# Layer two's projections as seven block products of scaled float16 pairs in a two-layer decoder trunk

## The chip, the cores and the metric

The kernel runs on one core of one Trainium2 chip. The metric is the device time of one execution in microseconds (us), lower is better. Engines are named as the profile names them: PE is TensorE (PEld its weight loads), DVE is VectorE, ACT is ScalarE, POOL is GpSimd, SP is SyncE, whose queue issues the DMAs.

## The reference

Two decoder layers over 1024 tokens of width 1024 (batch 1), all in float32. Layer one mixes by causal pooling, layer two by gated "forgetting" attention over keys and values that are projected once from layer one's result. Both also attend to 256 memory tokens. Cut to what matters:

```python
def mixer_sublayer(x, mem, w_in, w_mem_kv, w_out, main_fn):
    h = x @ w_in                       # columns [main | mem q | main gate | mem gate]
    u_main, q_mem, g_main, g_mem = ...  # 1024, 512, 1024, 512 columns
    y_main = main_fn(u_main)
    y_mem = memory_attention(q_mem, mem, w_mem_kv)
    y = jnp.concatenate([y_main * jax.nn.silu(g_main), y_mem * jax.nn.silu(g_mem)], axis=-1)
    return y @ w_out

def reference(...):
    for layer in range(2):
        if layer == 0: main_fn = causal_multiscale_pool      # windows 2, 4, 8, 16
        else:
            k, v, cum = shared_kv(x, w_kv_shared, b_forget)  # 1024 + 1024 + 16 columns
            main_fn = forgetting_attention(k, v, cum)        # 16 heads of 64, causal, logit + cum[t] - cum[s]
        y = mixer_sublayer(x, mem, w_in[layer], w_mem_kv[layer], w_out[layer], main_fn)
        x = layer_norm(ALPHA * x + y, ln_g[layer], ln_b[layer])
```

## The kernel before

**Products.** Every float32 operand is a pair: a large part rounded to fp32r and a small part in bfloat16 (`hi_lo`: ACT casts the large part, L187, DVE subtracts, L188). A product of two operands is three matmuls, large by large in fp32r and two crossed ones in bfloat16 (`three`).

**Slabs.** A projection is cut into slabs of 128 output columns (`slab`, its matmuls are L253). A slab is 2 halves of 512 tokens x 8 blocks of 128 along the inner dimension x 3 = 48 matmuls with 512 columns each, accumulated in one of two banks `pj`. Its weights come in two DMAs of 256 KB into `raw` and are split into `w` and `wl`; while attention runs, the flag `low` gives both steps of the split to POOL (`gp_hi_lo`, L197, L198). Layer two has 38 slabs: 8 of memory queries and gates, 8 of keys, 8 of queries, 6 of values, 8 of gates. The values of the first two pairs of heads and the forget gates come from `v_first` (L733), with tokens as rows.

**Stages.** Layer one: four pooling groups (each two slabs of values, the pooling on DVE, two slabs of gates, and a small product L231), with the memory attention after the first, then the output projection (`OutProj`, L486) in row blocks of 256 tokens x 3 parts of 48 matmuls, `norm` (L537 to L550) and the transposes that make layer two's x (L348, ACT and POOL split it again). Layer two: memory keys and values, four slabs of memory queries, the memory attention (`probs` L388 to L399) with the gates' slabs between its products, then the start (keys and queries of pair 0, keys of pair 1, `v_first`, forget gates), then FoX, then the output projection.

**FoX.** `fox` runs over 16 heads x 8 query tiles. For a tile, `probs` makes the logits (L231, two fp32r matmuls for each part of at most 512 keys, into one of three banks `L`), DVE adds the forget rows and takes the extreme (L871), ACT exponentiates into one of two banks `T` (L879), and a tile later `inverse_of` (DVE, L889 to L892) and `halves` write the large half (ACT, L900) and the small half (DVE, L901) of the probabilities, which a transposing DMA (L913) turns for the product with the values (L926, L932, bank `O`, evacuated by L938 on ACT and L939 on DVE). POOL masks the rows (L863). Key and query slabs are evacuated by an ACT cast and a DVE subtraction on 64 partitions for each half head (L782, L783 and L792, L793); the swapped copies of the keys are made by DMA. Between these steps `fill.pump` puts a share of the coming slabs' matmuls on PE.

**Order.** PE's order is written out by hand (`manual_schedule`, and in FoX the constants SHARE, FRAC and LAG). The other engines' orders and the DMA queue's are laid by the framework's scheduler when the kernel is built. `OutProj.open` hands each row block four banks, from `pj`, `L`, `T` and `O` in turn.

## Time and profile before

| | |
|---|---|
| runs | 1224.68, 1230.59, 1228.9 us; median 1228.9 |
| profiled execution | 1224.89 us, its span 1223.2 us |
| granted PE clock | 0.997 |
| HBM read / written | 94.97 MB / 22.61 MB |

How to read the views: the busy time of a group of instructions is given with its count and the mean of one in ns, and behind a second bar the idle time of its engine just before it with what ended most of it. A matmul's own duration contains the time that its result takes to come out, so the pace is read from the starts of neighbours. A row of the waits says which engine and line waited, for which, how long in total, how many times, and the longest.

### The profile page before, as it was taken

To read this page: it belongs to the slowest core of one execution; us is meant where nothing else is said; L and a number is where in the kernel's file an instruction comes from. 1 tells how busy PE (TensorE), PEld (TensorE's weight loads), DVE (VectorE), ACT (ScalarE), POOL (GpSimd) and SP (SyncE) were. 2 spreads that over 40 slices of the span, in tenths; PEclk is the share of its full clock that TensorE was granted. 3 is DMA by queue.
4 is the path that set the end of the run, shared out by engine and by line. 5 is a ranking of instruction groups with operands and counts; after the bars stand their busy time and mean duration, and the time that the engine had idled before them with its cause. 6 is when DMAs were issued, how large, how long until landed. Compare 5 with 4: busy or idle time off the path is not lost. (4 is left out here: it accounts for less than half of the span.)

```text
span 1223.2 us, 19702 instructions
## 1 busy us (share of the span) xinstructions
PE 1193.1 (98%) x7018; PEld 749.0 (61%) x7018; DVE 787.3 (64%) x1861; ACT 607.2 (50%) x1318; POOL 201.8 (16%) x312
## 2 busy tenths in 40 slices
PE   9999999999999998999999999999999999999996
PEld 4567665555556557566775656666666666655553
DVE  6544776375554458257555878777878878775653
ACT  6433754263421135156334777767766777683110
POOL 2000000000000004000004334433334324530000
PEclk9999999999999999999999999999999999999998
DMA  6332454243363235224528698868887879975430
GB/s 238 115 104 93 115 121 147 87 121 97 126 208 104 103 104 190 69 77 99 173 64 167 161 177 182 194 148 188 184 178 174 185 175 226 232 232 175 163 113 35
DMA packets 267410, 178.65 MB, mean 146 GB/s; under 512 B 212272, under 2 KB 225712, under 8 KB 267312
## 3 DMA queue, kind: packets, MB, share of 16 engines
q1 hardware_dynamic: 267312, 177.40, 55.1%
q8 instruction: 55, 0.90, 0.3%
q14 instruction: 43, 0.35, 0.1%
HBM read 94.97 MB, written 22.61 MB: 96 GB/s over the span
## 5 line engine op out<-in xcount | busy, mean ns | idle before, releaser
L253 PE MATMUL pj<-A,w 128*128 128x512 bf16 (+1 forms) x1952 | 618.1, 398 | 2.2 <-DVE MK L340 0.9
L253 PE MATMUL pj<-A,wl 128*128 128x512 bf16 x976 | 369.1, 380 | 0.3 <-POOL A L192 0.3
L253 PEld LDWEIGHTS pj<-A,w 128*128 128x128 f32 x976 | 180.7, 188 | 46.0 <-ACT A L187 1.7
L253 PEld LDWEIGHTS <-w 128*128 128x128 bf16 x992 | 95.8, 98 | 123.8 <-issue 36.3
L253 PEld LDWEIGHTS <-wl 128*128 128x128 bf16 x992 | 97.4, 98 | 94.3 <-issue 6.1
L879 ACT ACTIVATE T<-MK,s 128x512 f32<-128x512 f32 x192 | 111.0, 578 | 57.1 <-DVE s L871 36.3
L901 DVE SCALAR_TENSOR_TENSOR P<-T,s,P 128x512 f16<-128x512 f32 x192 | 111.9, 613 | 32.8 <-ACT P L900 31.4
L900 ACT ACTIVATE P<-T,s 128x512 f16<-128x512 f32 x192 | 102.6, 575 | 51.2 <-issue 27.5
L188 DVE TENSOR_TENSOR wl<-raw,w 128x512 bf16<-128x512 f32 x98 | 71.0, 728 | 82.3 <-ACT w L187 81.7
L486 PEld LDWEIGHTS <-T 128*128 128x128 bf16 x736 | 70.8, 98 | 86.5 <-issue 3.9
L231 PE MATMUL L<-B,B 128*128 128x512 f32 (+3 forms) x384 | 110.8, 390 | 4.1 <-DVE s L871 3.8
L187 ACT CAST w<-raw 128x512 fp32r<-128x512 f32 x106 | 64.7, 617 | 99.8 <-PE pj L253 71.5
L231 PEld LDWEIGHTS L<-B,B 128*128 128x128 f32 x384 | 70.6, 189 | 30.7 <-DVE s L871 11.3
L192 POOL TENSOR_SCALAR A<-A 128x512 bf16<-128x512 f32 (+1 forms) x20 | 17.0, 866 | 433.5 <-ACT A L187 433.5
L871 DVE CUSTOM_DVE_ANT_0 MK<-L,R 128x512 f32<-128x512 f32 (+3 forms) x128 | 72.7, 568 | 8.1 <-DMA R<-cumd 4.4
L863 POOL TENSOR_SCALAR_AFFINE_SELECT R<-R 128x128 f32<-128x128 f32 x128 | 41.5, 330 | 212.5 <-DVE s L871 112.8
L187 ACT CAST T<-T 128x1024 fp32r<-128x1024 f32 x23 | 24.0, 1045 | 98.5 <-DMA T<-y1d 53.3
L198 POOL TENSOR_TENSOR wl<-raw,w 128x512 bf16<-128x512 f32 x54 | 69.1, 1280 | 3.5
L188 DVE TENSOR_TENSOR T<-T,T 128x1024 bf16<-128x1024 f32 x23 | 29.0, 1261 | 41.6 <-ACT T L187 21.7
L197 POOL TENSOR_SCALAR w<-raw 128x512 fp32r<-128x512 f32 x54 | 34.3, 634 | 71.6 <-PE pj L253 71.6
L231 PE MATMUL pj<-T,w 128*128 128x256 bf16 (+1 forms) x256 | 44.3, 281 | 1.5 <-DVE MK L340 1.5
L926 PE MATMUL O<-T,V 128*128 128x128 f16 x576 | 38.2, 219 | 4.9 <-DMA T<-P 4.9
(255 smaller groups left out, 1732.7 us busy)
## 6 DMA issues: line engine op xcount, KB each, us to landing
raw<-in_win_dram SPq DMA_DIRECT2D x96, 256.0 KB, 2.8
raw<-in_wout_dram SPq DMA_DIRECT2D x40, 256.0 KB, 2.7
B<-B SPq DMA_DIRECT2D x32, 256.0 KB, 4.4
R<-cumd SPq DMA_DIRECT2D x16, 512.0 KB, 4.3
y0d<-Y SPq DMA_DIRECT2D x12, 512.0 KB, 2.8
T<-y0d SPq DMA_DIRECT2D x12, 512.0 KB, 3.9
T<-y1d SPq DMA_DIRECT2D x11, 512.0 KB, 3.8
raw<-in_wmk_dram SPq DMA_DIRECT2D x16, 256.0 KB, 2.6
```

Source lines behind the costliest of these rows:

```text
L187: pin(nc.scalar.copy(hi, src))
L188: pin(by.tensor_tensor(lo[0], src, hi.bitcast(F32), ALU.subtract))
L198: nc.gpsimd.tensor_tensor(lo[0], src, hi.bitcast(F32), ALU.subtract)
L231: nc.tensor.matmul(acc, a, b, start=i == 0, stop=i == len(terms) - 1)
L253: nc.tensor.matmul(acc, a, b, start=start, stop=stop)
L486: nc.tensor.matmul(acc, y, w, start=c == 2 and j == firsts[id(acc)], stop=c == 1 and j == lasts[id(acc)])
L863: nc.gpsimd.affine_select(R[:, qs], R[:, qs], [[-1, P]], ALU.is_ge, -NEG, base=0, channel_multiplier=1).ins
L871: nc.vector.tensor_tensor_reduce(p[:, lo:up], lg, R[:, lo:up], 1.0, top, ALU.add, ALU.min, m[:, n : n + 1])
L879: nc.scalar.activation(e, p[:, lo:up], AF.Exp, bias=top, scale=-1.0, accum_out=sums[:, n, hd % 2, i : i + 1],)
L900: nc.scalar.activation(pair[:, lo:up], e, AF.Copy, scale=r)
L901: nc.vector.scalar_tensor_tensor(pair[:, L + lo : L + up], e, r, pair[:, lo:up], ALU.mult, ALU.subtract)
L926: nc.tensor.matmul(acc[:, cols(i)], v[:, b, 2 * j : 2 * j + 2, :].rearrange("p e d -> p (e d)"), pt[hd, i][:, j, :], start=n == 0, stop=Fa ...
```

## The change

Layer two's slabs are computed two at a time. The 1024 inner rows and the 2 x 128 columns of two slabs form 2 x 2 blocks of the weights, and x, with the inner dimension and the tokens cut in halves, 2 x 2 blocks too. Instead of 8 block products of 12 matmuls there are 7 (`strassen`, the form of Winograd with four sums on each side), whose results are combined in PSUM and in a tile U: a copy from bank to bank, two copies to U on ACT, two additions on DVE. All operands of these products are pairs of float16 parts, scaled by powers of two; the scales go back in where results leave PSUM.

- The four sums of x (T1 to T4) are made by POOL behind `norm`, and transposed with the four plain blocks (`turned`): 128 transposes where there were 64.
- The sums of the weight blocks are made in layer one by `prepass`, 20 groups, one started every 8 steps (`tick`) of PE's written order: four loads, a pass on ACT that measures the size, a small matmul that shares it over the partitions, a scaling on DVE, sums and halves on POOL and ACT, and seven stores of 256 KB to DRAM (`wd`). In layer two, `Stream` loads the blocks, four ahead.
- FoX has 14 groups, in the order FOX_GROUPS and to the goals TARGETS. The weight splits on POOL, the late gates and their reloads are gone. The swapped keys are made by POOL copies instead of DMAs.
- Banks: `pj` 3 (were 2), `L` 3, `T` 2; `O` is gone, its users take `L`. `raw`, `w` and `wl` share ten buffers.
- The rows of layer one's output projection go in blocks s and s + 4; `v_first` stands ahead of the memory queries and uses float16 pairs; the start has one group (keys and queries of pair 0). Layer one's keys and values of memory are called from the same code, and layer two's memory parts are loaded during layer one's last step.
- The scheduler lays the other engines' orders against another timing model (`schedule_with_timeline_sim=True`).

```diff
+ORDER = (B11, T1, T2, B21, T3, B22, T4)
+AHEAD = 4
+PERIOD = 8
+GROUP = 84 * NH
+PART = 12 * NH
+TARGETS = [2 * (p + 1) * GROUP + PART for p in range(5)] + [int(n * GROUP) for n in (11.6, 13.2, 14)]
...
+        def measure(m, first, raws):
+            for j, r in enumerate(raws):
+                r = flat(r)
+                nc.scalar.activation(junk[:, : r.shape[1]], r, AF.Abs, accum_out=m[:, first + j : first + j + 1])
...
+        def shared(diag):
+            t = ps([P, 4, P], "T", 2)
+            nc.tensor.matmul(t[:, 0, :], ones_b, diag, start=True, stop=True)
+            return t
...
+        def scale(k, t, raws):
+            e, sc = tiny(1), tiny(1)
+            nc.vector.tensor_reduce(e, t[:, 0, :], AX.X, ALU.max)
...
+            for r in raws:
+                nc.vector.tensor_scalar(r, r, sc, None, ALU.mult)
+        def large(src):
+            t = pre([P, 2, *src.shape[1:]], F16)
+            nc.scalar.copy(t[:, 0], src)
+            return t
+        def small_part(t, src):
+            nc.gpsimd.tensor_tensor(t[:, 1], src, t[:, 0], ALU.subtract)
+        def both(src):
+            t = pre([P, 2, *src.shape[1:]], F16)
+            nc.gpsimd.tensor_scalar(t[:, 0], src, 1.0, 1.0, ALU.mult, ALU.mult)
+            small_part(t, src)
+            return t
+        def group(k):
...
+            a11, a12, a21, a22 = r
+            s1 = pre()
+            nc.gpsimd.tensor_tensor(s1, a21, a22, ALU.add)
+            t22 = large(a22)
+            small_part(t22, a22)
+            yield
+            t11 = large(a11)
+            ts1 = both(s1)
+            yield
+            nc.sync.dma_start(wd[k, 6], t22)
+            nc.gpsimd.tensor_tensor(a21, a11, a21, ALU.subtract)
+            small_part(t11, a11)
...
+    def strassen(stream, XB, U, evac, straight=None, done=None):
+        def part(acc, k, fresh):
+            w = stream.block()
+            for kt in range(4):
+                for j, (a, b) in enumerate(((0, 0), (1, 0), (0, 1))):
+                    nc.tensor.matmul(
+                        acc, w[:, a, kt, :], XB[b][:, ORDER[k], kt, :], start=fresh and kt == 0 and j == 0,
+                        stop=kt == 3 and j == 2, skip_group_check=True,
+                    )
...
+        def summed(f, acc):
+            dst = straight(f) if straight else U[:, f, :]
+            nc.vector.tensor_tensor(dst, acc, U[:, f, :], ALU.add)
+            if not straight:
+                evac(f, slice(NH, S), dst)
+        b1 = bank()
+        yield from part(b1, 0, True)
+        b2 = bank()
+        nc.scalar.copy(b2, b1)
+        b3 = bank()
+        yield from part(b3, 1, True)
+        nc.scalar.copy(U[:, 1, :], b3)
+        yield from part(b2, 2, False)
+        nc.scalar.copy(U[:, 0, :], b2)
+        yield from part(b1, 3, False)
+        evac(0, slice(0, NH), b1)
+        yield from part(b2, 4, False)
+        summed(1, b2)
+        yield from part(b3, 5, False)
+        summed(0, b3)
+        yield from part(b2, 6, False)
+        evac(1, slice(0, NH), b2)
...
-            turned = ((pj, pj, l, l), (t, t, l, o)) if self.l else ((pj, pj, l, l), (l, o, pj, pj), (l, l, l, o))
+            turned = ((pj, l, pj, l), (t, t, pj, l)) if self.l else ((pj, l, pj, l),)
...
+    def turned(sp, zs, XB, sums):
+        (p0, p1), (s0, s1) = ((z[:, :NH], z[:, NH:]) for z in zs)
+        t1, t2, t3, t4 = sums
+        nc.gpsimd.tensor_tensor(t1, s0, p0, ALU.subtract)
+        nc.gpsimd.tensor_tensor(t2, s1, t1, ALU.subtract)
+        nc.gpsimd.tensor_tensor(t3, s1, s0, ALU.subtract)
+        nc.gpsimd.tensor_tensor(t4, p1, t2, ALU.subtract)
+        def turn(src, k):
+            t = ps([P, 4, P], "T", 2)
+            for j in range(4):
+                nc.tensor.transpose(t[:, j, :], src[:, j * P : (j + 1) * P], ident)
+            at = slice(None), k, slice(None), slice(sp * P, (sp + 1) * P)
+            nc.scalar.activation(XB[0][at], t, AF.Copy, scale=sx)
+            nc.vector.scalar_tensor_tensor(XB[1][at], t, sx, XB[0][at], ALU.mult, ALU.subtract)
...
-                        for to, of in ((own, other), (other, own)):
-                            nc.sync.dma_start(w[to, :].bitcast(F32), t[of, :].bitcast(F32))
+                for t, w, (own, other) in zip(ks, ws, halves) if f == 0 else ():
+                    for to, of in ((own, other), (other, own)):
+                        nc.gpsimd.tensor_scalar(w[to, cols], t[of, cols].bitcast(F32), 1.0, 1.0, ALU.mult, ALU.mult)
...
-            acc = ps([P, NH], "O", 1)
+            acc = ps([P, NH], "L", 3)
...
-    with _tile.TileContext(nc) as tc:
+    with _tile.TileContext(nc, schedule_with_timeline_sim=True) as tc:
```

More of the change, by code (lines that the diff above doesn't have):

```diff
@@ new lines, in trunk_kernel, with __init__, ahead, block @@
+    class Stream:
+        def __init__(self, groups):
+            self.blocks = [wd[k, i] for k in groups for i in range(7)]
+            self.tiles, self.n = [], 0
+        def ahead(self, upto):
+            for b in self.blocks[len(self.tiles) : upto]:
+                self.tiles.append(wt([P, 2, 4, P], F16))
+                nc.sync.dma_start(self.tiles[-1], b)
+        def block(self):
+            self.n += 1
+            self.ahead(self.n + AHEAD)
+            return self.tiles[self.n - 1]
@@ L376, in probs @@
+        ys = [ytile() for _ in range(MH)]
         def probs(i):
@@ L498, in early, with rest @@
             yield from self.products(self.accs, 2, yh, yl)
-        def rest(self, resid, XH, XL, dst):
-            self.split(24)
+        def rest(self, resid, XB, dst, last=None):
             gb = []
@@ L841, in start_units @@
             yield from own
-            complete(0)
         masked = []
```

676 lines of the change are left out of this document (433 added, 243 removed).

## The prediction

> **What bounds the kernel now.** I read four views, from coarse to fine: the page, the table of busy time by stage, the waits of each engine inside the longest stage, and the timeline of TensorE. From the page:
>
> ```profile
> span 1223.2 us, 19702 instructions
> PE 1193.1 (98%) x7018; PEld 749.0 (61%) x7018; DVE 787.3 (64%) x1861; ACT 607.2 (50%) x1318; POOL 201.8 (16%) x312
> ```
>
> TensorE looks like the bound everywhere. The stages, cut at layer one, layer two's memory attention, the start of its main path, the 128 attention tiles (FoX below), and the output projection (columns: stretch, length, then busy us and count of PE, PEld, DVE, ACT, POOL, the granted clock, DMA share, GB/s):
>
> ```profile
> 14.00:480.00 466.00, 463.61 (x2476) 284.58 (x2474) 271.39 (x496) 186.76 (x364) 20.90 (x24) 1.00 0.39 123
> 490.00:594.00 104.00, 104.00 (x642) 65.31 (x642) 54.23 (x134) 50.70 (x139) 0.00 (x0) 1.00 0.36 87
> 594.00:657.00 63.00, 63.00 (x408) 45.33 (x407) 30.30 (x75) 18.18 (x35) 4.46 (x7) 1.00 0.46 127
> 657.00:1081.00 424.00, 412.82 (x2752) 266.68 (x2750) 337.63 (x974) 300.89 (x699) 160.98 (x264) 1.00 0.84 185
> 1081.00:1223.00 142.00, 130.94 (x648) 75.93 (x648) 77.43 (x138) 34.63 (x59) 8.11 (x8) 0.98 0.42 140
> ```
>
> In the first three and the last, VectorE (DVE) is busy at most 58% of the time and TensorE all of it: there a matmul saved is time saved. FoX is different: DVE is busy 80%, ScalarE (ACT) 71%, the DMA engines 84%. Its waits from 645 to 1080 us (engine and line, what it waited for, us in total, times, longest; 11 rows for DVE, first two and last shown; three of ACT's, two of PE's):
>
> ```profile
> DVE P L901 <- ACT P L900: 31.4, 50, 1.1
> DVE s L889 <- ACT T L879: 25.7, 31, 1.6
> ...
> DVE MK L871 <- issue: 0.3, 1, 0.3
> ACT T L879 <- DVE s L871: 36.3, 33, 3.0
> ACT B L782 <- PE pj L253: 6.8, 2, 3.4
> ACT B L792 <- PE pj L253: 2.7, 1, 2.7
> PE O L926 <- DMA T<-P: 4.9, 4, 2.1
> PE L L231 <- DVE s L871: 3.8, 11, 0.7
> ```
>
> None of DVE's 11 rows names PE: the logits are always there before DVE reduces them (L871), and it is PE that waits for DVE to empty a bank. ACT's waits for PE come to 9.5 us. So FoX turns at the pace of the loop reduce (DVE), exp (ACT), inverse (DVE), high half (ACT), low half (DVE), with TensorE close behind. The Trainium skill (Perfetto Trace Analysis, Identifying the Most-Contended Engine) says that the busy share of matmul rows is no measure of how near TensorE is to its limit; these waits agree.
>
> **The change part by part.** The sum is made against the profiled run: 1224.9 us, its span of 1223.2 and 1.7 around it; the median of the three runs, 1228.9, lies 4.0 above it.
>
> *Matmuls.* From TensorE's timeline (start, length): where two slabs that follow each other begin, and two bfloat16 products of one slab with 13 between them:
>
> ```profile
> 510.44 1.51 PE L253 MATMUL pj<-A,w 128*128 128x512 f32 x5
> 521.06 1.51 PE L253 MATMUL pj<-A,w 128*128 128x512 f32 x5
> ...
> 511.79 0.38 PE L253 MATMUL pj<-A,wl 128*128 128x512 bf16 x1
> 514.81 0.38 PE L253 MATMUL pj<-A,wl 128*128 128x512 bf16 x1
> ```
>
> And a piece of the chain that ended last, matmuls of float16 pairs with 128 columns:
>
> ```profile
> 1082.52 1.47 PE O L926 x26
> ```
>
> A slab of 48 matmuls takes 521.06 - 510.44 = 10.62 us; bfloat16 matmuls of 512 columns follow each other every (514.81 - 511.79) / 14 = 0.2157 us; the fp32r third is slower, which makes up the rest. Float16 runs at the bfloat16 pace: 26 of 128 columns in 1.47 us are 0.0565 each, a quarter of 0.2157 and a little. A pair of slabs goes from 2 x 10.62 = 21.24 us to 84 x 0.2157 = 18.12. With 38 slabs as 19 groups: 403.6 - 344.3 = 59.3 us less for TensorE. By stage: memory attention, four groups, 85.0 - 72.5 = 12.5; the start, where three slabs (keys and queries of pair 0, keys of pair 1) become one group, 31.9 - 18.1 = 13.8; FoX, 27 slabs become 14 groups, 286.7 - 253.7 = 33.0. In the first two TensorE is the bound, so these 26.3 us count in full; the copies between the seven products have a distance of 12 matmuls, 2.6 us, against about 0.6 us on ACT.
>
> *Transposes.* Eight fp32 transposes, and the matmul behind them:
>
> ```profile
> 480.12 1.04 PE L348 MATMUL T<-ident,G 128*128 128x128 f32 x8
> 481.03 0.27 PE L231 MATMUL pj<-T,w 128*128 128x256 bf16 x1
> ```
>
> They take 481.03 - 480.12 = 0.91 us. The turned sums T1 to T4 add 64 transposes to the 64: +7.3 us, all on TensorE's path. Twenty small matmuls that share a group's maximum add 20 x 0.0565 = 1.1. Two edits I cost at nothing. The last row block's eight transposes wait for its norm and for POOL's four sums; ahead of most of them stand the memory keys and values, 8 x 24 matmuls of 256 columns, about 8 x 24 x 0.108 = 21 us; without that cover it would be some 5. The first output projection leaves one free bank of each kind per row block, and needs the second after 8 matmuls; the one it takes has been closed 24 matmuls, 5.2 us, before the block ends.
>
> *FoX on DVE and ACT.* The combinations and copies cost as these rows do (line, engine, operation, shapes, count, busy us, mean ns of one):
>
> ```profile
> L537 DVE SCALAR_TENSOR_TENSOR G<-G,L 128x512 f32<-128x512 f32 x8 | 5.4, 679 | 13.2 <-PE L L486 13.2
> L819 ACT COPY MK<-pj 128x512 f32<-128x512 f32 x12 | 6.8, 570 | 0.0
> L783 DVE TENSOR_TENSOR B<-pj,B 64x512 fp32r<-64x512 f32 x26 | 17.9, 689 | 1.2 <-ACT B L782 0.2
> L782 ACT CAST B<-pj 64x512 fp32r<-64x512 f32 x25 | 14.4, 574 | 4.9 <-DVE B L783 4.2
> ```
>
> DVE gains two sums per group, 28 x 0.68 = 19.0, and the evacuation of pair 1's keys, which moves in from the start, 4 x 0.69 = 2.8: 21.8 us, to 359. ACT gains three copies per group, 42 x 0.57 = 23.9, loses 6 value copies (3.4) and takes on 4 casts (2.3): +22.8. The weight splits that go were POOL's already, so neither engine gets anything back. The bounds: if FoX followed TensorE it would lose 33.0; if every added DVE operation came on top it would gain 21.8. I take -9.5: the 32 added DVE operations of 0.68 us fit the 81 gaps of 0.6 to 0.8 in which DVE waits for ACT (31.4 / 50 and 25.7 / 31), and so cost nothing net, and the 9.5 us that ACT waits for PE go, since PE will be further ahead. What is late next is the loop itself. Values now take a bank from the logits' three, about once in four tiles; the 2.6 us that PE then loses at most have the 33 us as cover. The keys' swapped copies go from 32 DMAs to 64 half-width POOL copies; POOL has 161 of 424 us busy and loses 101 of it with the splits, and the wider weight blocks (14 x 1.79 MB for 27 x 0.5 MB) take the place of those DMAs in the queue.
>
> *Layer one.* The prepass runs here beside a TensorE that is full. POOL is idle now (20.9 of 466 us). Its rows, ACT's for the measuring pass, and the first and last of 16 groups of DVE operations that read two tiles from SBUF:
>
> ```profile
> L198 POOL TENSOR_TENSOR wl<-raw,w 128x512 bf16<-128x512 f32 x54 | 69.1, 1280 | 3.5
> L197 POOL TENSOR_SCALAR w<-raw 128x512 fp32r<-128x512 f32 x54 | 34.3, 634 | 71.6 <-PE pj L253 71.6
> ...
> L187 ACT CAST w<-raw 128x512 fp32r<-128x512 f32 x76 | 46.6, 618 | 77.5 <-PE pj L253 54.0 <-PE pj L231 12.7 <-issue 4.4
> ...
> L188 DVE TENSOR_TENSOR wl<-raw,w 128x512 bf16<-128x512 f32 x71 | 51.8, 734 | 61.1 <-ACT w L187 60.9
> ...
> L188 DVE TENSOR_TENSOR Y<-raw,Y 128x512 bf16<-128x512 f32 x4 | 2.6, 684 | 0.0
> ```
>
> A group has 11 two-input and 4 one-input operations on POOL: 11 x 1.28 + 4 x 0.63 = 16.6 us. It starts every 8 steps; a pool group has 20 steps in 4 x 10.62 + 24 x 0.2157 = 47.7 us, so 19.1 us a group; the output projection 4 in 48 x 0.2157 = 10.35, so 20.7, with 3.4 us of the turned sums in it. POOL is then filled to 87% and 97%: 341 us in all with the sums. ACT gets seven passes of about 0.62, 19 x 4.3 = 82 us, to 269 of 466: no bound. DVE gets four scalings (no row has them; between 0.2 and 0.7 us, I take 0.4 as an estimate from the 0.68 of two-input rows) and about 1.4 us of small steps: 20 x 3 = 60, to 331 of 466. But the two share something (start, length, engine):
>
> ```profile
> 477.87 1.28 POOL L188 TENSOR_TENSOR wl<-raw,w 128x512 bf16<-128x512 f32 x1 [1.93 <-ACT w L187]
> ...
> 478.34 1.35 DVE L188 TENSOR_TENSOR wl<-raw,w 128x512 bf16<-128x512 f32 x1
> ```
>
> A DVE subtraction that takes 0.68 alone takes 1.35 when it starts under a POOL addition, and ends 0.54 after it: it waited for the whole of it. Layer one's 16 such groups hold 223 operations and 186 us, with the scalings 303. POOL runs 341 / 466 = 73% of the time, and half an operation is 0.64: 303 x 0.73 x 0.64 = 142 us of waiting, which brings DVE to 473 of 466. Two queues pass this on. In PE's written order the sharing matmul waits for the measuring pass, and the slabs stand behind it. On SP's queue seven stores of a group wait for POOL, and the slabs' weight loads stand behind them, with one slab (10.6 us) loaded ahead; the bytes themselves, 19 x 2.8 MB in 466 us or 114 GB/s, double the 123 at a DMA share of 0.39, which still fits. So I charge layer one +10; the bounds are 0 (the waits fall in DVE's idle time) and +60 (below). The Trainium skill (SBUF — State Buffer, Who interferes with whom) has it as a rule: VectorE and GpSimd share a pair of ports, and an operation that needs them blocks the other for its whole length. By that rule the +60 applies; the pair of rows agrees.
>
> Sum: 1224.9 - 12.5 - 13.8 + 7.3 + 1.1 - 9.5 + 10 = 1207.5. Two of three runs lay 4.0 and 5.7 above the profiled one, so I add 2.5: **1210**.
>
> **The rivals.** *TensorE sets the pace throughout.* DVE's 86 us of gaps in FoX close, and layer one hides the prepass: 1224.9 - 59.3 + 8.4 + 2.5 = 1176.5. For it: FoX needs only 359 us of DVE for 391 of PE, and the filled gaps. Against: DVE never waited for PE. Chance 0.24.
>
> *POOL and DVE exclude each other in layer one (the other side).* In a pool group of 47.7 us POOL needs 2.5 x 16.6 = 41.5; DVE's two-input operations take about 19 to 26, the scalings 4; taking off the overlap of 0.14 us (0.68 - 0.54) at each of some 70 changes leaves 55 to 61, so 7 to 13 too much: 30 over three groups; in the output projection about 8 per row block of 31 us, 32 over four. TensorE feels it through the sharing matmuls and late splits: +60 in place of +10, 1260. It decides once a prepass group takes longer than its 19.1 us. For it: the pair of rows. Against: the gate stage has room, and the lag may run on into the next. Chance 0.17.
>
> *FoX's loop takes every added operation.* +21.8 in place of -9.5: 1241. For it: the fixed order of DVE and ACT; against: the 81 gaps. Chance 0.10.
>
> **How the numbers follow.** The forecast keeps 0.49, with its own range 1190 to 1232 (FoX by -29 to +12). The range, **1176 to 1245**, takes in the first rival and the third and leaves out most of the second and some of the edges, 0.19. A change under 0.5% (1222.8 to 1235.0) can't be told from none. Faster: 0.24 and 0.40 of the forecast's 0.49, 0.64. Same: 0.06 of it and 0.03 of the third, 0.09. Slower: 0.27.
>
> **What would show it.** L253 falls to 1152 matmuls, the new product line has 1596 at 0.216 us. Memory attention and start lose 26 us together. FoX: DVE's waits still name ACT, and its busy share rises to 86% or so; if they name PE, the first rival has it; if FoX is over 430 us, the third. Layer one: DVE's 0.68 us subtractions read 0.9 to 1.4, and PE has waits on DVE or POOL of about 10 us; if these reach 50, the second. The forecast is wrong if layer one or FoX is off by over 25 us.

## The result, and the profile after

The changed kernel takes 1371.3 us (median of 3 runs, 1364.4 to 1371.4) where the kernel before takes 1228.9: 1.1147 times as long, 95% interval 1.1094 to 1.12. The prediction was 1210 with a range of 1176 to 1245. The profiled run took 1364.4 us, 139.5 more than that of before. The experiments below are one execution each, but for the last three kernels, which have four. The changed kernel's page:

```profile
span 1362.7 us, 20716 instructions
PE 1201.6 (88%) x6874; PEld 711.9 (52%) x6874; DVE 958.0 (70%) x2141; ACT 712.1 (52%) x1547; POOL 524.9 (39%) x558
```

TensorE's share fell from 98% to 88%, and VectorE gained 171 us, GpSimd 323. Where this sits is seen when both kernels are cut at the same events: the first memory query product of layer two, the first and the last reduce of FoX, the end. First the kernel before, then the changed one (stretch, length, busy us and count of PE, PEld, DVE, ACT, POOL, granted clock, DMA share, GB/s):

```profile
14.00:489.30 475.30, 470.51 (x2534) 290.55 (x2531) 278.83 (x518) 192.22 (x374) 23.78 (x27) 1.00 0.39 124
489.30:656.70 167.40, 167.40 (x1049) 111.14 (x1049) 85.08 (x208) 68.88 (x174) 4.24 (x6) 1.00 0.40 102
656.70:1082.20 425.50, 413.77 (x2757) 267.28 (x2755) 338.98 (x978) 302.09 (x701) 161.76 (x265) 1.00 0.84 185
```

```profile
14.00:566.00 552.00, 484.53 (x2395) 284.23 (x2393) 414.84 (x728) 259.92 (x550) 391.92 (x307) 0.94 0.62 200
566.00:632.70 66.70, 54.57 (x420) 45.32 (x421) 27.39 (x71) 20.57 (x42) 14.13 (x10) 0.92 0.43 130
632.70:767.50 134.80, 124.02 (x757) 69.22 (x755) 76.26 (x175) 59.28 (x144) 6.32 (x10) 0.96 0.52 130
767.50:1217.30 449.80, 394.86 (x2626) 232.26 (x2626) 356.13 (x1003) 327.98 (x737) 105.41 (x219) 0.95 0.82 177
```

The change also moved the first values ahead of the memory queries. In the kernel before they stand behind them, as one row of TensorE's timeline:

```profile
601.73 23.07 PE L733 MATMUL L<-MK,A 128*128 128x272 f32 x192
```

So 489.3 of before compares as 489.3 + 23.1 = 512.4. The four parts, with what the prediction had for each:

| part | before | after | difference | predicted |
|---|---|---|---|---|
| up to the first memory query product (with the first values) | 512.4 | 632.7 | +120.3 | +18.4 (10 + 7.3 + 1.1) |
| memory attention and start, to the first reduce | 144.3 | 134.8 | -9.5 | -26.3 |
| FoX, first to last reduce | 425.5 | 449.8 | +24.3 | -9.5 |
| the rest | 141.0 | 145.4 | +4.4 | 0 |

These sum to 139.5. In FoX, the answer to the rows of DVE's and PE's waits in the prediction (the first four of DVE's 14, the first two of PE's six):

```profile
DVE P L1267 <- ACT P L1266: 24.5, 37, 2.6
DVE s L1255 <- ACT T L1245: 16.9, 21, 1.6
DVE MK L1237 <- PE L L233: 16.5, 20, 2.8
DVE G L1305 <- ACT G L1304: 11.7, 12, 2.2
...
PE L L1292 <- DMA T<-P: 23.3, 9, 5.2
PE pj L485 <- DVE B L1143: 15.7, 7, 3.1
```

VectorE now waits 16.5 us for logits, which no row named before, and TensorE waits for the transposing DMAs (23.3 us in place of 4.9) and for VectorE to empty a bank. VectorE is busy 17.1 us longer and idle 7.2 us longer: together the 24.3. In layer one, VectorE's and GpSimd's groups from 14 to 566 us (busy us, mean ns of one):

```profile
L189 DVE TENSOR_TENSOR w<-w,w 128x512 bf16<-128x512 f32 x63 | 61.8, 984 | 26.3 <-ACT w L188 22.8 <-PE pj L255 3.4
L374 DVE TENSOR_SCALAR pre<-pre,s 128x512 f32<-128x512 f32 x80 | 42.7, 597 | 0.9
...
L382 POOL TENSOR_TENSOR pre<-pre,pre 128x512 f16<-128x512 f32 x137 | 184.0, 1357 | 39.6 <-ACT pre L378 39.2
...
L420 POOL TENSOR_TENSOR pre<-pre,pre 128x512 f32<-128x512 f32 x19 | 39.0, 2054 | 98.2 <-DVE pre L374 83.0 <-DVE s L662 15.2
```

A subtraction of a slab's split, 0.73 us on average before, reads 0.98, and GpSimd's 1.28 reads up to 2.05. Worked out from all its instructions there, each against the fastest twentieth of its form, VectorE's instructions hold 96 us of stretching (7 before) in 456 us, GpSimd's 79 in 399; these are sums of single lengths, some of which overlap.

One more column has moved: the granted clock, 1.00 in the first three stages before, reads 0.92 to 0.96 after. In these traces it stands at 1.0 or at 0.5 and nowhere between, so a mean of 0.95 over FoX's 449.8 us means some 45 us at half of it. The changed kernel's TensorE around a wait in the start, and the busy times and the clock of 10.3 us that begin within that wait:

```profile
739.22 5.77 PE L485 MATMUL pj<-A,w 128*128 128x512 f16 x26
750.23 0.77 PE L1113 MATMUL L<-G,G 128*128 128x128 f32 x2 [5.24 <-DVE G L1109]
750.79 3.01 PE L1115 MATMUL L<-G,G 128*128 128x112 f32 x14
753.64 3.15 PE L485 MATMUL pj<-A,w 128*128 128x512 f16 x7
```

```profile
747.00:757.30 10.30, 7.07 (x26) 4.91 (x27) 4.17 (x8) 0.18 (x1) 0.93 (x2) 0.50 0.45 74
```

Before the wait 26 matmuls take 5.77 us, 0.22 each; behind it seven take 3.15, 0.45 each. The changed kernel's trace has 26 such stretches of 3.4 to 10.3 us, and before each of them TensorE sat idle for at least 1.8 of 3.4 us. The kernel before has none until its end. TensorE is busy for 58 us of them up to the first memory query product and for 36 us in FoX. By the doubled time of a matmul about half of that is lost, 29 and 18 us; this is an estimate, of TensorE's time and not of the stages'. A wait here costs more than its own length, and all differences below contain this.

### The profile page after: what moved, and what is told of

Its sections match the earlier page's. It is cut to its first block, busy times and chain, and to the rows that moved or that the text cites. A ratio compares the mean times of both kernels' runs of the same rounds, so it can differ in the third digit from the quotient of the medians.

```text
span 1362.7 us, 20716 instructions
## 1 busy us (share of the span) xinstructions
PE 1201.6 (88%) x6874; PEld 711.9 (52%) x6874; DVE 958.0 (70%) x2141; ACT 712.1 (52%) x1547; POOL 524.9 (39%) x558
## 5 line engine op out<-in xcount | busy, mean ns | idle before, releaser
L485 PE MATMUL pj<-A,w 128*128 128x512 f16 x1596 | 383.6, 384 | 17.8 <-DVE B L1143 15.7
L255 PE MATMUL pj<-A,w 128*128 128x512 bf16 (+1 forms) x1104 | 263.8, 401 | 8.6 <-DVE w L189 3.0
L485 PEld LDWEIGHTS <-w 128*128 128x128 f16 x1596 | 143.5, 99 | 185.0 <-issue 31.3
L382 POOL TENSOR_TENSOR pre<-pre,pre 128x512 f16<-128x512 f32 x138 | 184.4, 1350 | 39.6 <-ACT pre L378 39.2
L255 PEld LDWEIGHTS <-w 128*128 128x128 bf16 x768 | 70.7, 100 | 99.6 <-issue 26.1
L189 DVE TENSOR_TENSOR w<-w,w 128x512 bf16<-128x512 f32 x74 | 69.4, 940 | 33.7 <-ACT w L188 29.9
L1237 DVE CUSTOM_DVE_ANT_0 MK<-L,R 128x512 f32<-128x512 f32 (+3 forms) x128 | 72.5, 569 | 22.4 <-PE L L233 16.3
L188 ACT CAST w<-w 128x512 fp32r<-128x512 f32 x82 | 50.3, 617 | 70.9 <-DMA w<-in_win_dram 42.4
L255 PEld LDWEIGHTS pj<-A,w 128*128 128x128 f32 x368 | 69.6, 192 | 23.6 <-DVE Y L531 3.0
L386 POOL TENSOR_SCALAR pre<-pre 128x512 f16<-128x512 f32 x76 | 68.7, 907 | 4.3 <-DMA wd<-pre 4.0
L758 PEld LDWEIGHTS <-w 128*128 128x128 bf16 x368 | 36.7, 100 | 59.1 <-DVE w L189 10.4
L350 ACT ACTIVATE junk<-pre 128x512 bf16<-128x512 f32 (+1 forms) x81 | 50.5, 624 | 26.8 <-DMA pre<-in_win_dram 17.9
L233 PE MATMUL L<-T,w 128*128 128x256 bf16 (+1 forms) x384 | 51.5, 297 | 12.5 <-ACT w L188 9.1
```

Source lines behind the costliest of these rows:

```text
L189: pin(by.tensor_tensor(lo[0], src, hi.bitcast(F32), ALU.subtract))
L233: nc.tensor.matmul(acc, a, b, start=i == 0, stop=i == len(terms) - 1)
L255: nc.tensor.matmul(acc, a, b, start=start, stop=stop)
L350: nc.scalar.activation(junk[:, : r.shape[1]], r, AF.Abs, accum_out=m[:, first + j : first + j + 1])
L382: nc.gpsimd.tensor_tensor(t[:, 1], src, t[:, 0], ALU.subtract)
L386: nc.gpsimd.tensor_scalar(t[:, 0], src, 1.0, 1.0, ALU.mult, ALU.mult)
```

## Experiments: layer one

Here I compare the time of the first memory query product: 512.4 us in the kernel before (as shifted above), 632.7 in the changed kernel. The theory: the prepass's arithmetic on GpSimd and VectorE's operations exclude each other. Rivals: stores that wait on SyncE's queue, the transfers themselves, the planner's order, or something outside the prepass.

**No prepass but for one group (e5).**

```diff
-todo = [group(k) for k in [V_OF, MQ_OF, ..., KQ_OF] + [k for k, _ in FOX_GROUPS]]
+todo = [group(k) for k in [V_OF, MQ_OF]]
-self.blocks = [wd[k, i] for k in groups for i in range(7)]
+self.blocks = [wd[MQ_OF, i] for k in groups for i in range(7)]
```

> Leaves out: the prepass makes only the blocks of the first values and of one group; all 19 groups then read that one group's blocks and scale. Everything behind layer one has the same instructions and bytes. Theory (the prepass costs layer one its 119 us, up to the first memory query product at 632.7 us): that product comes at 515 to 530 us (489.3 of before and some 23.5 for the first values, which the change moved ahead of it, and up to 15), total 1245 to 1260 us, and VectorE loses its 96 us of stretched instructions. Rival (the merged buffers of weights, the changed banks and the output projection's new loading cost layer one its time, not the prepass): the product stays behind 580 us. On the FoX stage both say nothing: its 467 us stay within 8.

The product comes at 541.5, total 1267.3. So 91 us of the 120 are the prepass's, and 29 are not (or are those of the two groups left: the first values and one more), more than the theory allowed. They are seen where the same events cut this run and the kernel before: 10.5 up to the output projection's first product (the two groups run there), 6.2 in it (132.0 to 138.2: 36 more transposes, some 4 us at 0.114 each), and 12 behind it, where TensorE's largest waits are

```profile
PE L L233 <- ACT w L188: 6.9, 4, 3.0
PE L L233 <- POOL w L189: 2.2, 2, 1.1
PE T L867 <- DVE A L870: 1.6, 1, 1.6
```

for the splits of the memory keys' and values' weights and for the last transposes, which now all stand between two layers with nothing else to multiply. FoX takes 441.7 us here, 8.1 less than in the changed kernel with the same code there (the 467 us of the expectation are cut 17 us later); its section comes back to this. More telling is the total: **even with a prepass that costs next to nothing the kernel is slower than before.**

**One pair in place of all sums and splits (e3).**

```diff
-a11, a12, a21, a22 = r      # 3 copies on ScalarE, 15 operations on GpSimd, 7 stores
-...
+t = large(r[3])
+small_part(t, r[3])
+for i in (6, 1, 0, 4, 3, 2, 5):
+    nc.sync.dma_start(wd[k, i], t)
```

> Leaves out: per prepass group, all sums and all splits but one; the pair of the lower right block is stored seven times. Loads, measuring, scaling and stored bytes stay; GpSimd has 1 operation per group in place of 15, ScalarE 1 copy in place of 3. Theory (GpSimd's arithmetic, by excluding VectorE and by holding stores, makes the 119 us): the first memory query product comes at 520 to 550 us in place of 632.7, total 1250 to 1285. Rival (the loads, the bytes stored, or the measuring and scaling on ScalarE and VectorE make them): the product stays behind 590 us.

The product comes at 571.2, some 20 us behind the theory's window but far from the rival's, total 1303.2. The arithmetic, with whatever waits for its results, costs 632.7 - 571.2 = 61.5 us; the loads, the measuring, the scaling and the stores cost the 29.7 between 571.2 and 541.5.

**The same, with GpSimd's work back as dead work (g1).** This tells exclusion from waiting for results, since nobody reads what GpSimd writes.

```diff
+for j in range(...):                       # 11 in a group
+    nc.gpsimd.tensor_tensor(dead_h[:, 1], dead, dead_h[:, 0], ALU.subtract)
+...                                        # and 4 nc.gpsimd.tensor_scalar
```

> Leaves out what e3_one_pair left out, and its last subtraction; then GpSimd gets its 11 two-input and 4 one-input operations per group back, but as dead work on a scratch tile that nothing reads and nothing waits for. Theory (GpSimd's operations block VectorE's through what the two share): the first memory query product comes at 610 to 640 us, like the 632.7 of the changed kernel and unlike e3_one_pair's 571.2, and VectorE's SBUF-to-SBUF operations are stretched by 80 us or more. Rival (stores, buffers and the sharing matmul that wait for GpSimd's results cost the 61 us): the product stays at 560 to 585.

The product comes at 665.7, 94.5 us later than with one pair and later than in the changed kernel. VectorE's same two groups, without and with the dead work:

```profile
L189 DVE TENSOR_TENSOR w<-w,w 128x512 bf16<-128x512 f32 x63 | 43.5, 692 | 24.1 <-ACT w L188 19.1 <-PE pj L255 3.4 <-PE L L233 1.3
L374 DVE TENSOR_SCALAR pre<-pre,s 128x512 f32<-128x512 f32 x80 | 39.6, 557 | 1.1 <-DVE s L371 0.3
```

```profile
L374 DVE TENSOR_SCALAR pre<-pre,s 128x512 f32<-128x512 f32 x80 | 73.2, 975 | 0.5
L189 DVE TENSOR_TENSOR w<-w,w 128x512 bf16<-128x512 f32 x63 | 70.0, 1113 | 12.6 <-ACT w L188 11.1 <-PE pj L255 1.3
```

0.69 becomes 1.11 us and 0.56 becomes 0.98 (134 us of stretching in all, 19 without). Work that nobody waits for costs more than the work it stands for. TensorE's waits name GpSimd for only 9 us, so the exclusion is shown as a cause. Its share of the 61.5 us is not: dead work starts whenever GpSimd is free, and so meets more of VectorE's scalings (L374) than the real work, which waits for them. The run also makes the pair's small half by a ScalarE copy and gives the prepass 9 buffers in place of 11. And some 28 of the 94.5 us are slower matmuls: TensorE is busy at half the clock for 78 us here and for 22 with one pair (half of the difference, estimated as above).

**Stores from GpSimd's queue (e4).**

```diff
-nc.sync.dma_start(wd[k, 6], t22)
+nc.gpsimd.dma_start(wd[k, 6], t22)         # and the other six of a group
```

> The 133 stores of weight blocks are issued from GpSimd's own queue, behind the arithmetic that they wait for, in place of SyncE's, where the slabs' weight loads stand behind them. Theory (stores that wait for GpSimd hold SyncE's queue for 210 us, and the weights come late): the first memory query product moves from 632.7 to under 585 us, and ScalarE's waits for win (40.9 us) fall under 10. Rival (GpSimd and VectorE exclude each other and GpSimd is simply full): the product stays within 20 us of 632.7 or comes later, since GpSimd now issues 133 transfers as well.

The product comes at 687.4, total 1417.9: 55 us worse. In the changed kernel SyncE's queue waits for GpSimd 210 us in layer one, yet taking these waits off the weights' queue does not help; the run adds 47 us to GpSimd's busy time and 45 to VectorE's stretching, so it shows no more than that taking the waits off SyncE in this way is no gain; what they cost stays open.

**The planner's setting off (e1).**

```diff
-with _tile.TileContext(nc, schedule_with_timeline_sim=True) as tc:
+with _tile.TileContext(nc) as tc:
```

> Only the planner's setting that the change switched on (it orders instructions by a simulated timeline) is switched off again. Theory (the cost is in the work that was added, whatever the order): total within 15 us of 1371. Rival (the order that the planner writes makes the cost, in layer one or in FoX): total under 1340 us, with FoX under 445 us or the first memory query product before 600.

1455.0 us, the product at 728.3. Both views missed: the order matters much, but the change's order is the better one. The prediction had not priced this edit.

**The arithmetic on VectorE and ScalarE (g2).**

```diff
-nc.gpsimd.tensor_tensor(t[:, 1], src, t[:, 0], ALU.subtract)
+nc.vector.tensor_tensor(t[:, 1], src, t[:, 0], ALU.subtract)
-ts1 = both(s1)                             # GpSimd rounds; now ScalarE (large), VectorE (small_part)
+ts1 = large(s1); small_part(ts1, s1)
```

> The changed kernel with the prepass's arithmetic moved off GpSimd: the 11 sums and subtractions of a group go to VectorE (0.68 us each alone, 1.28 on GpSimd), the four roundings to ScalarE. The result is the same. Theory (GpSimd's work costs layer one by stretching VectorE's, 96 us): VectorE has some 360 + 150 us of work of its own for a stage of 550, nothing is stretched, and the first memory query product comes at 575 to 605 us in place of 632.7. Rival (VectorE is then the bound itself): 630 or later.

The product comes at 604.7, total 1336.1, 28 us under the changed kernel's fastest run. VectorE is busy 477 of 591 us, with 17 of stretching, so one engine doing all of it beats two that block each other. It is still no gain over the kernel before.

**No measuring and scaling (e6)**, on top of the one pair in place of all sums and splits.

```diff
-measure(m, 0, r[:2])
+if k == V_OF:
+    measure(m, 0, r[:2])                   # and so for the sharing matmul and the scaling
```

> Like e3_one_pair (one pair per prepass group in place of all sums and splits), and the measuring on ScalarE (82 us), the scaling on VectorE (40 to 60 us) and the sharing matmul left out too, but for the first values; loads and stores of the same bytes stay. The first memory query product comes at 571.2 in e3_one_pair and at 541.5 without the prepass. Theory (ScalarE, VectorE and the matmul that waits for them make the 30 us between): 543 to 553. Rival (the transfers do: 19 x 2.8 MB, and SyncE's queue): 563 to 572.

The product comes at 636.9, total 1376.8: neither. The edit took away what paced the prepass, and its transfers ran at once. DMA's busy share and GB/s in the 40 slices of its page, 34.4 us each:

```profile
DMA  6699997553234523361376698789888678767321
GB/s 225 186 380 384 382 390 228 108 138 115 77 123 147 176 93 111 109 201 47 100 146 172 141 196 178 167 188 196 197 178 172 140 172 175 167 148 232 131 81 58
```

From 70 to 200 us they move 380 to 390 GB/s, and TensorE waits 77 us for splits whose weights come late (`w`, L188). How the 29.7 us divide between measuring, scaling and transfers stays open.

## Experiments: FoX

Compared is the time from the first to the last reduce: 425.5 before, 449.8 after. The theory: VectorE's loop takes each operation that the seven products add. Rivals: ScalarE's copies, the place of TensorE's fill, the transposing DMAs. How far FoX varies with the same code in it is seen in the runs above that changed layer one alone: 441.7 us with one group of the prepass (its row below), 443.7 with the dead work, 447.7 with the stores on GpSimd's queue, 448.2 with the arithmetic on VectorE, 448.9 with one pair. A difference of up to 8 us between two single runs is therefore not clear of this.

```profile
677.40:1119.10 441.70, 392.35 (x2626) 230.95 (x2626) 356.45 (x1006) 327.49 (x737) 104.98 (x219) 0.95 0.83 180
```

**No sums, no copies (f1); no sums alone (f3); no copies alone (f4).**

```diff
-nc.vector.tensor_tensor(dst, acc, U[:, f, :], ALU.add)     # f1, f3: left out
-nc.scalar.copy(b2, b1)                                      # f1, f4: left out,
-nc.scalar.copy(U[:, 1, :], b3)                              # with the one of U[:, 0, :]
```

> Leaves out: the three ScalarE copies between the seven products of each group and the VectorE sums (22 of 28 in FoX; the six of the values become copies). The output halves are then single products. TensorE's matmuls are the same. Theory (FoX's loop of VectorE and ScalarE takes each added operation, the prediction's third rival): FoX, 449.8 us from the first to the last reduce against 425.5 before, falls to 420 to 435. Rival (TensorE's fill is placed too early, so that the logits and values come late): it stays within 6 of 449.8.

> Leaves out only VectorE's sums of products (22 of the 28 in FoX; the six of the values become copies). ScalarE's three copies a group stay. FoX takes 449.8 us from the first to the last reduce in the changed kernel and 426.6 with sums and copies both left out. Theory (VectorE's added operations alone set the difference): 426 to 433 us. Rival (ScalarE's added copies do): 442 to 450. Between the two, both share it.

> Leaves out only ScalarE's copies between products, from the second group on; VectorE's sums stay and add an old value. Theory (VectorE's added operations alone set the difference): FoX stays at 444 to 452 us. Rival (ScalarE's copies do): 426 to 434.

The stage of the three runs, in this order:

```profile
773.60:1200.20 426.60, 385.93 (x2626) 225.50 (x2626) 340.36 (x984) 304.42 (x695) 98.97 (x219) 0.96 0.87 186
```

```profile
770.60:1204.10 433.50, 386.83 (x2626) 225.48 (x2626) 341.21 (x982) 325.94 (x737) 99.34 (x219) 0.96 0.87 184
```

```profile
772.90:1226.60 453.70, 397.98 (x2626) 232.67 (x2626) 355.88 (x1003) 307.93 (x695) 105.65 (x219) 0.93 0.81 175
```

Without VectorE's sums FoX loses 16.3 us for the 15 that VectorE loses. Without ScalarE's copies alone it loses nothing (453.7, 2 over the theory's window); without both, 23.2. Without the additions, then, FoX takes as long as before the change, although TensorE is busy 28 us less (413.8 to 385.9): the matmuls saved there bought nothing. VectorE's two waits for ScalarE in the first of the three runs:

```profile
DVE P L1264 <- ACT P L1263: 25.4, 42, 1.3
DVE s L1252 <- ACT T L1242: 18.0, 26, 1.6
```

They are 43.4 us without sums and copies, 47.2 without the sums and 41.4 with all of them: of 15 us of sums some 6 went into these gaps, but VectorE's waits for the logits grew by as much, from 10.4 us without the sums to 16.5. The clock has a part here that no run separates: TensorE is busy at half of it for 36 us in the changed kernel and for 19 in each of the two runs without sums.

**A third of FoX's slab matmuls left out, in the kernel before (h1).**

```diff
-put(acc, a, b, j == 0, j == len(order) - 1)
+if not low[0] or j % 3 != 1:               # low[0] holds in FoX
+    put(acc, a, b, j == 0, j == len(order) - 1)
```

> The kernel before with a third of the matmuls of FoX's slabs left out (the same third of each slab; the paces of everything else are as they were): TensorE loses some 90 us of its 412.8 in FoX, three times what the change saves there. Theory (FoX goes at the pace of VectorE's and ScalarE's loop, and matmuls saved there are worth nothing): FoX takes 415 to 425 us from the first to the last reduce, in place of 425.5, total over 1218. Rival (TensorE is the second bound close behind, as the first rival of the prediction and the forecast's 9.5 us had it): under 410, total under 1212.

1231.2 us beside 1230.0 for the kernel before on the same chip:

```profile
655.50:1084.90 429.40, 347.88 (x2298) 232.60 (x2328) 331.74 (x972) 297.71 (x695) 159.65 (x263) 0.90 0.87 181
```

```profile
DVE MK L872 <- PE L L231: 20.8, 18, 3.2
...
PE O L927 <- DMA T<-P: 61.5, 26, 4.9
```

TensorE is busy 66 us less and the stage is no shorter. TensorE comes earlier to the values that stand in its written order and stops there for the transposing DMA (61.5 us); the logits written behind them come late, and VectorE waits for TensorE, as it does in the changed kernel. So a wait on TensorE here does not mean that TensorE has too much to do. Why TensorE is busy only 66 us less, where 90 were expected, the granted clock of 0.90 tells: 61 us of its work run at half the clock, behind its waits, and take some 30 us longer (estimated as above). The run shows that matmuls left out do not shorten FoX in this written order. It does not show that the loop of VectorE and ScalarE alone would hold FoX at 425 us: neither another place of the values nor a full clock was tried.

**Half the transposed bytes**, in that kernel (h3) and in the changed one (f5).

```diff
-nc.sync.dma_start_transpose(pt[hd, i], two[:, : n * P])
+nc.sync.dma_start_transpose(pt[hd, i][:, : i + 1, :], two[:, : (i + 1) * P])
```

> Like h1_before_fewer (a third of the slabs' matmuls in FoX left out), and only the high halves of the probabilities are transposed by DMA; the low products read the high block again. Theory (the transposing DMAs are what FoX waits for once TensorE has less): FoX falls from 429.4 to 410 or less, and TensorE's 61.5 us of waits for them to under 20. Rival (the loop of VectorE and ScalarE alone sets the pace): 418 to 432, whatever TensorE waits for.

> The changed kernel with only the high halves of the probabilities transposed by DMA; the low products read the high block again. Theory (FoX's added 24 us come from the transposing DMAs, which share SyncE's queue and the DMA engines with wider weight blocks): FoX falls from 449.8 to 425 - 437. Rival (they come from VectorE's added sums): it stays within 7 of 449.8, and TensorE's 23.3 us of waits for the DMAs go elsewhere.

```profile
658.30:1086.30 428.00, 351.69 (x2330) 232.24 (x2328) 331.75 (x972) 300.06 (x696) 158.32 (x266) 0.91 0.62 139
```

```profile
767.90:1208.40 440.50, 393.52 (x2626) 231.02 (x2626) 354.37 (x1003) 326.98 (x737) 104.72 (x219) 0.95 0.60 139
```

The DMA share falls to 0.62 and 0.60, and the stages to 428.0 from 429.4 and to 440.5 from 449.8. The DMA engines' bytes set no floor, and TensorE still waits 42.4 us for the transposes in the first of the two runs, where under 20 were expected. In the changed kernel the transposes' bytes have a part of at most 9 of the 24 us, and 9.3 is hardly more than FoX varies with the same code. That run lies between its two expectations.

**Fill spread evenly (f2).**

```diff
-TARGETS = [2 * (p + 1) * GROUP + PART for p in range(5)] + [int(n * GROUP) for n in (11.6, 13.2, 14)]
+TARGETS = [int(n * GROUP) for n in (1.75, 3.5, 5.25, 7, 8.75, 10.5, 12.25, 14)]
```

> The 14 groups are spread over the eight pairs of heads evenly, 1.75 a pair, in place of 2 for each of the first five and less then; the keys go ahead of the values and gates to be in time. Theory (added VectorE and ScalarE operations set FoX's time): FoX stays within 6 of 449.8 us. Rival (the first pairs are bound by TensorE, 55 us a pair, and the last by the loop): FoX falls to 425 to 440, and VectorE's 16.4 us of waits for the logits fall under 8.

465.5, 15.7 worse: the even fill is refuted as a cure; why it costs that much was not followed up.

## Experiments: a better version

**The planner's setting in the kernel before** (e2; the edit of e1 the other way round).

> The kernel before with the one setting of the change that costs no instruction: the planner orders by a simulated timeline. In the changed kernel that setting is worth 84 us (1455.0 without it). Theory (it helps only where there is a prepass to order around, since TensorE's order is written by hand and TensorE is full): within 8 us of 1229. Rival (it helps any order): 1205 to 1220.

1228.3 beside 1226.8: nothing.

**Less VectorE work, and a slab from the start into FoX, in the kernel before.**

```diff
-nc.vector.scalar_tensor_tensor(dst, dst, 1.0, acc, ALU.add, ALU.mult)
+u = raw([P, NH])                           # v1, v2: inside FoX
+nc.scalar.copy(u, acc)
+nc.gpsimd.tensor_tensor(dst, dst, u, ALU.mult)
+nc.gpsimd.tensor_tensor(dst, dst, u, ALU.add)
...
-own = chained((keys, 48), (queries, 48), (following, 48))
+own = chained((keys, 48), (queries, 48))   # v3, v2: the second pair's keys go to fox()
```

> The kernel before, with the gates inside FoX taken off VectorE: its 16 operations of 0.68 us (10.9 us) become a ScalarE copy (0.57) and two GpSimd operations (1.28 each, 41 us of GpSimd's 263 idle ones). Theory (FoX goes at the pace of VectorE's operations, ScalarE's copies cost nearly nothing there): FoX 425.5 to 414 - 420, total 1217 to 1224 beside 1228. Rival (ScalarE shares the loop's pace, or GpSimd's operations hold VectorE's and the tiles): within 4 of the kernel before, or over it.

> The kernel before, with the keys of the second pair of heads (one slab, 10.6 us of TensorE) moved from the start into FoX, a gate slab from FoX's first pair to its second, and the first values at the head of the start. Theory (TensorE has slack in FoX): the start loses 6 to 10 us (the chain of the forget gates, 31 us from the first values to the first reduce, then bounds it), FoX gains 3 to 6 (four operations of VectorE, 2.8 us): total 1222 to 1228. Rival (a slab in FoX costs what it costs elsewhere): FoX gains 10 or more, total 1228 or over.

> The two edits of v1_gates_off_vector and v3_keys_only together. Theory (they do not touch each other): the sum of both gains, 1212 to 1222. Rival (GpSimd's gates and the fuller first pairs collide): no better than the better of the two.

All slower, by 1 to 2%: v1 1244.2 us, ratio 1.0135 (1.0119 to 1.015), v3 1238.9, 1.0095 (1.008 to 1.011), v2 1254.2, 1.021 (1.0193 to 1.0227), beside 1227.8. In v1, FoX took 442.6, and VectorE's waits say why:

```profile
DVE MK L877 <- POOL R L869: 20.7, 14, 4.7
```

(4.5 us before.) GpSimd masks each tile's forget row in order, and the gates' operations of 1.28 us now stand ahead of the mask that the next reduce needs. So the theory that VectorE's operations alone set FoX's time fell: they cost time when added, but GpSimd, whose masks stand in that ring, has no room to take them over in this order (TensorE, too, waits 8.7 us for GpSimd's splits of weights there). In v3 the start became 1.5 us shorter, of the 10.6 moved out of it, and FoX 13.3 longer. The first reduce waits for the forget gates:

```profile
622.83 0.17 DVE L736 TENSOR_TENSOR G<-L,bfb 128x16 f32<-128x16 f32 x1 [2.68 <-ACT T L735]
...
655.33 0.69 DVE L871 CUSTOM_DVE_ANT_0 MK<-L,R 128x512 f32<-128x512 f32 x1 [4.07 <-DMA R<-cumd]
```

32.5 us from the last first value to the first reduce, through some 20 operations of VectorE, two matmul steps and two transfers, whatever TensorE does meanwhile. No run beat the kernel before.

## Why the prediction was wrong, step by step

- **Matmul prices, right.** L253 (now L255) is left with layer one, the new line L485 has 1596 matmuls, and the first 90 take 19.59 us; less the 0.38 of the last one's own length that is (19.59 - 0.38) / 89 = 0.2158 each, as the 0.2157 of the bfloat16 rows had it. This holds at the full clock. That matmuls behind a wait take twice as long (29 us of TensorE's time in layer one and 18 in FoX, estimated) stands in no term of the sum.

```profile
632.74 19.59 PE L485 MATMUL pj<-A,w 128*128 128x512 f16 x90
```

- **Memory attention, right:** cut where the start's first slab or group begins (595.0 before, 726.4 after) it goes from 105.7 to 93.7 us, -12.0 for the -12.5.
- **"These 26.3 us count in full", wrong for the start:** it takes 61.7 us before, 38.6 without the first values; these 38.6 become 41.1, not 24.8. I read TensorE's full row as the only bound there. Below it ran the chain of the forget gates, 31 us to the first reduce, with the first values and three slabs as cover; with them gone TensorE waits 5.2 us inside that chain (`PE L L1113 <- DVE G L1109: 5.2, 1, 5.2`) and the first reduce waits for the chain's end. v3 shows the same floor in the kernel before.
- **"The 32 added DVE operations fit the 81 gaps and so cost nothing net", wrong.** The gaps are the latency of a ring (reduce, exp, inverse, high, low). They did shrink, from 57.1 us to 41.4 in the two rows of VectorE's waits for ScalarE, but others opened, 16.5 us for the logits and 11.7 in place of 2.2 behind ScalarE's evacuation (G L1305), and VectorE's 17.1 us of added work came on top. VectorE's additions cost 16.3 us for 15 by f3, and with ScalarE's copies 23.2 by f1, each give or take the 8 us by which FoX varies. The third rival, with its 21.8 and a chance of 0.10, had the direction and the operations: FoX came to 449.8, past its mark of 430. That 21.8 fits 24.3 so well is in part luck, since it has neither the new waits nor the half clock.
- **"The 9.5 us that ACT waits for PE go", wrong:** after the change the two largest of them are 11.3 us (G L1304) and 9.0 (A L508), 20.3 together. And h1 shows that matmuls taken from FoX's slabs do not shorten it, though TensorE's row was 97% full. The prediction had quoted the waits that say so (DVE never waits for PE) and drew half the conclusion. The first rival fell with it.
- **"I charge layer one +10", wrong, the largest miss.** The second rival's mechanism, exclusion, was right. Its +60 fits the 61.5 of e3 in part by luck: it had 30 us in the pooling groups and 32 in the output projection, where e3 finds 39.6 up to the output projection's first product, 17.0 in the projection and 4.9 behind it, and e3 takes away the waits for GpSimd's results as well. I gave it a chance of 0.17 although its own sum had the prepass over its time in every pool group, and bounded layer one by the same 60, as if nothing could come on top. The Trainium skill (SBUF — State Buffer, Who interferes with whom) says that the later of two such operations is fully blocked; e3 and g1 agree, 0.69 us against 1.11. The four scalings, estimated at 0.4 us, take 0.56 each where nothing stretches them. Another 30 us are the rest of the prepass (e3 against e5), which the sum had at nothing because ScalarE and VectorE had room; what of it is transfers is open.
- **The cover for the last transposes, half wrong:** the memory keys and values stand there as named, but TensorE waits some 10 us for their splits, so the cover is full of holes.
- **Rivals treated as alternatives.** The second and the third both came true, and they add: 1207.5 + 50 + 31.3 = 1289. That is still 76 short of 1364.4: the rest of the prepass (30), the start (16), what lies outside the prepass in layer one (29 where 8 were priced), the last stage (4) and 5 of small differences make it up. (One reading of mine was off without touching the sum: in the last stage of the kernel before, TensorE is busy 131 of 142 us, not all of it.)

## What to carry to other kernels

Before pricing a saved matmul, leave some out and see whether the stage gets shorter: a TensorE row that is 97% full moved the end by nothing when it lost 66 us, since TensorE then waited for the transposing DMA and ran at half its clock behind these waits. In a ring of VectorE, ScalarE and a DMA an added operation can cost about its length even where gaps of its size are listed. A wait of TensorE of about 2 us or more is to be priced above its length. Idle time of GpSimd is not free room while VectorE works SBUF to SBUF. Rivals that rest on different stages are to be summed, not weighed against each other.

## What the runs showed of the hardware that I had not expected

VectorE's operations that read one operand from PSUM are not stretched, while SBUF-to-SBUF ones next to them are:

```profile
266.55 1.15 DVE L189 TENSOR_TENSOR w<-w,w 128x512 bf16<-128x512 f32 x1
267.13 1.70 POOL L432 TENSOR_TENSOR pre<-pre,pre 128x512 f32<-128x512 f32 x1
267.63 0.67 DVE L531 SCALAR_TENSOR_TENSOR Y<-Y,pj 128x512 f32<-128x512 f32 x1
```

The gate's multiplication (L531) takes its 0.67 us wholly under a GpSimd addition (its 16 of this form in layer one all take 0.67 to 0.69), the subtraction before it 1.15 in place of 0.69. And even VectorE's scaling by one column (L374), with a single SBUF operand, went from 0.56 to 0.98 us beside GpSimd's dead work. The Trainium skill (same section) says both: at most one SBUF input does not contend, unless the operation is of a kind that can take both ports, scaling among them. By these rows the room that the prepass had lay at VectorE's operations on PSUM; no run places GpSimd's work there.

The granted clock fell with TensorE's waits, from 0.997 on average to 0.946 in the changed kernel, to 0.922 with the planner's setting off and to 0.961 in h1, where TensorE had less to do. Such a mean is easily read as a sign of waiting and no more. It is a cost as well: it is made of stretches at 0.5, and in them matmuls of 512 columns start every 0.43 us in place of 0.22, in the changed kernel and in h1 alike. No run keeps TensorE busy through its waits, so what the half clock costs a whole stage stays open.
